# First layer of a two-layer network with a PEER expert layer: all 128 expert columns multiplied ahead of the value pass, sums of the value pass in eight PSUM banks

## The chip, the cores and the metric

The kernel runs on one core of a Trainium2 chip. The metric is the time of one execution on the device in microseconds (us), as the median over runs; a profile of one execution shows what each engine did. The engines are TensorE (PE, with its weight loads as PEld), VectorE (DVE), ScalarE (ACT), GpSimd (POOL) and SyncE (SP), which only issues transfers (DMA).

## The reference, cut to what matters

Each of two layers has a mixer part and then an expert part (PEER). The change lies in the expert part:

```python
q = (t @ wq).reshape(TOKEN_BLOCK, PEER_HEADS, 2, PEER_DK // 2)
s = jnp.einsum("thpd,hpnd->thpn", q, sub_keys)
st, it = lax.top_k(s, PEER_TOPK)
...
best, pos = lax.top_k(cand, PEER_TOPK)
e = jnp.take_along_axis(cidx, pos, axis=-1)
g = jax.nn.softmax(best, axis=-1)
u = jnp.take(eu, e, axis=0)
act = jax.nn.gelu(jnp.einsum("thkd,td->thk", u, t), approximate=False)
return jnp.einsum("thk,thkd->td", g * act, jnp.take(ev, e, axis=0))
```

There are 128 x 128 experts of width 1024. The first layer handles 512 tokens (256 context, 256 latent), the second only the 256 latent ones. Each layer's modulation vectors are silu(c) @ ada_w + ada_b.

## The kernel before, in words

Nothing is gathered. The experts are taken as 128 columns of 128 experts, and every column is computed for every token; a dense matrix G of gate weights, zero where an expert was not chosen, picks what counts. Three steps follow one another in a layer:

- **Routing** (`route`): the top-16 searches on DVE (phase 0), then the spread (phase 1), which makes G out of one-hot products: 128 steps in the first layer, each with one-hots from ACT, DVE and POOL, four short matmuls (L836) and two reductions on DVE (L838) into `rt_stg`, which goes to DRAM as G.
- **Inner products** (`inner`): for an expert column j the weights `u` are loaded, split into a high and a low part (`uh` on ACT, `ul` on POOL, L869 and L870) and multiplied with the split activations in three passes: 24 matmuls of 128x512 per column in the first layer (L887 to L889) into the PSUM tile `h`, then a gelu into a `ga` tile (L893). Columns below `NPRE` are woven into the routing: one each `EVERY` steps; their results go to DRAM (`act`).
- **Value pass** (`outer`): 64 steps of two columns. `weights` loads the gelu results back (`ga<-act`, tiles with three buffers), multiplies them with G (L965, DVE), and splits the product into `wh` (L968, ACT) and `wl` (L969, DVE). `values` loads the value rows `v` (two buffers) and splits them into `vh` (ACT) and `vl` (POOL for columns below `NPRE` in the first layer, else DVE). `second` multiplies: 512 tokens are four blocks `tt`, 1024 features two halves `k`, three passes, so 24 matmuls per column. Sums of blocks 0 and 1 stay in four PSUM banks (`acc`); those of blocks 2 and 3 go through two PSUM buffers (`f`) and are added on DVE to `accS` in SBUF (L1007). In the first layer columns 104 to 127 have their inner products here. `finish` turns each sum over, adds it to `x` and takes sums of squares.

While the first layer's value pass runs, `side` computes seven modulation vectors: 56 loads `wa`, each read by two DVE instructions `wtr` (L196), 112 in all. Each engine works its instructions off in a fixed order, and SP issues all these transfers in a fixed order too; a scheduler makes these orders from the program.

In the second layer 256 tokens make two blocks; all sums are in four banks already, and POOL has no part in the value pass.

Of the kernel before, what the change touches and what calls it, by code (L numbers as in the profile page):

```python
# [7 lines left out]
F32 = mybir.dt.float32  # L8
# [8 lines left out]
D = 1024  # L17
# [6 lines left out]
SPLIT = 3072.0  # L24
TG = 32
TT = 512
NPRE = (104, 96)
EVERY = ((3, 2), (2, 1))
UB = (5, 8)
UR = (2, 4)  # L30
VB = (5, 6)
# [18 lines left out]
class Net:  # L50
# [137 lines left out]
    def ada(self, l, P, w, cb, src):  # L188

        red = self.red()  # L190
        for b in range(NB):
            wt = self.wts.tile([128, D], F32, name="wa", tag="wt", bufs=2)
            self.nc.sync.dma_start(wt, src[b])
            for s in range(2):
                trash = self.wts.tile([128, D], BF, name="wtr", tag="whi", bufs=WB)
                self.nc.vector.scalar_tensor_tensor(trash, wt, 1.0, cb[:, s], op0=OP.mult, op1=OP.mult,  # L196
                                                    accum_out=red[:, b, s:s + 1])
            yield
        self.ada_out(l, P, w, red)

    def ada_half(self, l, P, w, acc, tags, banks, ctag):
# [694 lines left out]
    def peer(self, l, P, h, c0, npre, side):  # L896
        nc, I, tc = self.nc, self.I, self.tc
        n = TT - c0
        per = 512 // n
        NG = n // TG  # L900
        Gd = self.dram.tile([128, NG, 128, TG], F32, name=f"G{l}")
        Ad = self.dram.tile([npre // per, 128, 512], F32, name=f"act{l}")
        S = {}
        ups = ExitStack()
        pool = ups.enter_context(tc.tile_pool(name=f"expu{l}", bufs=2))
        with ExitStack() as rs:
            self.psum = rs.enter_context(tc.tile_pool(name=f"psr{l}", bufs=5, space=bass.MemoryType.PSUM))
            self.pbufs = {"f": 5}
            self.iotap = self.psum.tile([128, 128], F32, name="iotap", bufs=1)
            nc.vector.tensor_copy(self.iotap, self.iota)  # L910
            self.routep = rs.enter_context(tc.tile_pool(name=f"route{l}", bufs=1))
            def early():
                for j in range(npre):
                    a = self.inner(l, h, c0, j, per, pool, S, nc.gpsimd if LO[l][j % len(LO[l])] == "p" else nc.vector)
                    if a is not None:
                        nc.sync.dma_start(Ad[j // per], a)
                    yield
            pre = early()
            k = 0
            for phase in self.route(l, h, c0, Gd):  # L920
                if phase is None:
                    for _ in range(MORE[l]):
                        next(pre, None)
                    continue
                k += 1
                if k % EVERY[l][phase] == 0:
                    next(pre, None)
            for _ in pre:
                pass
        with ExitStack() as vs:  # L930
            self.psum = vs.enter_context(tc.tile_pool(name=f"psv{l}", bufs=2, space=bass.MemoryType.PSUM))
            self.pbufs = {"f": 2}
            X = vs.enter_context(tc.tile_pool(name=f"expv{l}", bufs=2))
            if l == 0:
                self.adap = vs.enter_context(tc.tile_pool(name="adap", bufs=1))
            self.outer(l, P, h, c0, npre, Gd, Ad, pool, X, S, side)
        ups.close()

    def outer(self, l, P, h, c0, npre, Gd, Ad, pool, X, S, side):
# [2 lines left out]
        per = 512 // n  # L942
        nt = n // 128
        V = I["peer_v"][l].rearrange("(i j) d -> i j d", j=128)
        acc = [self.psum.tile([128, 512], F32, name=f"acc{k}", tag=f"acc{k}", bufs=1) for k in range(4)]
        accS = X.tile([128, 4, 512], F32, name="accS", bufs=1) if nt > 2 else None
        st = {}

        def weights(n2):
# [21 lines left out]
                    r.append((wh[:, k * n:(k + 1) * n], wl[:, k * n:(k + 1) * n]))  # L971
            st["w", n2] = r

        def values(n2):
            r = []
            for j in (2 * n2, 2 * n2 + 1):
                v = X.tile([128, D], F32, name="v", tag="v", bufs=VR[l])
                nc.sync.dma_start(v, V[:, j, :])
                r.append(self.usplit(v, "v", X, VB[l], nc.gpsimd if j < npre and nt > 2 else nc.vector))
            return r  # L980

        def second(n2):
            vs = values(n2)
            ws = st.pop(("w", n2))
            order = [(tt, k) for tt in range(nt) for k in range(2)]
            if nt > 2:
                order = [(tt + d, k) for tt in (0, 1) for k in range(2) for d in (2, 0)]
            if n2 == last:
                order = [(tt, k) for tt in ((2, 0, 3, 1) if nt > 2 else (0, 1)) for k in range(2)]
            for tt, k in order:  # L990
                t = slice(tt * 128, tt * 128 + 128)
                if tt < 2:
                    A, s0, s1 = acc[2 * tt + k], n2 == first, n2 == last
                else:
                    A, s0, s1 = self.ps(), True, True
                for jj in range(2):
                    vh, vl = vs[jj][k]
                    wh, wl = ws[jj]
                    nc.tensor.matmul(A, wh[:, t], vh, start=s0 and jj == 0, stop=False)  # L999
                    nc.tensor.matmul(A, wh[:, t], vl, start=False, stop=False)  # L1000
                    nc.tensor.matmul(A, wl[:, t], vh, start=False, stop=s1 and jj == 1)  # L1001
                if tt >= 2:
                    o = accS[:, 2 * (tt - 2) + k]
                    if n2 == first:
                        nc.vector.tensor_copy(o, A)
                    else:
                        nc.vector.tensor_add(o, o, A)  # L1007
                if n2 == last:
                    finish(tt, k)

        def finish(tt, k):

            s = 0 if c0 + tt * 128 >= T else 1
            t = slice(c0 + tt * 128, c0 + tt * 128 + 128)
            sq = self.wts.tile([128, 512], F32, name="sq", tag="wlo", bufs=WB)
            if k == 0:
                st["ss", tt] = self.psum.tile([128, 128], F32, name="ss", tag="h", bufs=2)
            ss = st["ss", tt]
            if tt < 2:
                o = pool.tile([128, 512], F32, name="ga", tag="ga", bufs=3)  # L1020
                nc.scalar.activation(o, acc[2 * tt + k], AF.Copy)
            else:
                o = accS[:, 2 * (tt - 2) + k]
            pt = self.ps()
            for c in range(4):
                nc.tensor.transpose(pt[:, c * 128:(c + 1) * 128], o[:, c * 128:(c + 1) * 128], self.ident)
            for c in range(4):
                xs = self.x[:, 4 * k + c, t]
                nc.vector.scalar_tensor_tensor(xs, pt[:, c * 128:(c + 1) * 128],
                                               P["mod"][:, 5 * NB + 4 * k + c, s:s + 1], xs, op0=OP.mult, op1=OP.add)  # L1030
            nc.scalar.activation(sq.rearrange("p (c t) -> p c t", c=4), self.x[:, 4 * k:4 * k + 4, t], AF.Square)
            for c in range(4):
                nc.tensor.matmul(ss, self.ones, sq[:, c * 128:(c + 1) * 128], start=k + c == 0, stop=k + c == 4)
            eng = nc.vector if tt else nc.gpsimd
            if l == DEPTH - 1:
                if k == 0:
                    st["ys", tt] = self.wts.tile([128, NB, 128], F32, name="ys", tag="wt", bufs=2)
                ys = st["ys", tt]
                b = slice(4 * k, 4 * k + 4)
                eng.tensor_mul(ys[:, b], self.x[:, b, t], self.fg[:, b, None].to_broadcast([128, 4, 128]))  # L1040
            if k == 0:
                return
            self.rsqrt(ss, 1.0 / D, self.rsx[:, t], sq[:, :128])
            if l == DEPTH - 1:
                for b in (slice(0, 4), slice(4, 8)):
                    eng.tensor_mul(ys[:, b], ys[:, b], self.rsx[:, None, t].to_broadcast([128, 4, 128]))
                    nc.sync.dma_start(self.out[:, b, tt * 128:tt * 128 + 128], ys[:, b])
# [6 lines left out]
        for k in range(65):  # L1054
# [4 lines left out]
            if k < 64:  # L1059
                n2 = seq[k]  # L1060
                for j in (2 * n2, 2 * n2 + 1):
                    if j >= npre:
                        a = self.inner(l, h, c0, j, per, pool, S, nc.gpsimd if nt > 2 else nc.vector)
                        if a is not None:
                            st["a", j // per] = a
                weights(n2)
            if k:
                second(seq[k - 1])
            next(side, None)
            if k % 4 == 0:  # L1070
                next(side, None)


    def run(self):
# [111 lines left out]
```

## Time and profile before

| | us |
|---|---|
| median of 3 runs (lowest, highest) | 3119.13 (3117.34, 3130.06) |
| the profiled execution, own time | 3119.87 |
| its span in the trace | 3118.2 |
| PE busy in the span | 2933.3 (94%) |
| DVE, ACT, POOL busy | 2233.9, 1440.0, 1378.2 |

The span runs from the first to the last recorded instruction; 1.7 us of the execution lie around it. Busy shares are means over stages that differ; the rows below are read stage by stage. The first layer's routing takes some 430 to 1112 us of the span, its value pass 1127 to 2022, the second layer's value pass 2660 to 3110.

### The profile page before, as it was taken

The page shows a single profiled execution, that of the slowest core. Times are in us where ns is not written, and L with a number is a line of the kernel's source. Part 1 is how long each engine was busy: PE and PEld are TensorE (multiplying, and loading weights), DVE is VectorE, ACT ScalarE, POOL GpSimd, SP SyncE. Part 2 cuts the span into 40 slices and gives each one's busy share as a digit, 9 for nine tenths or more (in the row PEclk, how much of TensorE's full clock was granted, in tenths as well). Part 3 has the DMA queues.
Part 4 walks back from the last instruction along what each step waited for, and adds up shares of the span by engine and source line. Part 5 has one row for each costly group of instructions (what it writes and reads, how often), then busy time and mean ns, then how long its engine had stood idle before and what let it go on. Part 6 is the DMA issues. An engine that isn't in the chain of part 4 may idle for free.

```text
span 3118.2 us, 43562 instructions
## 1 busy us (share of the span) xinstructions
PE 2933.3 (94%) x14930; PEld 2424.5 (78%) x14930; DVE 2233.9 (72%) x4604; ACT 1440.0 (46%) x2861; POOL 1378.2 (44%) x1079
## 2 busy tenths in 40 slices
PE   7899989999999978989999999978989998999998
PEld 4476578888888856767888888867689998788887
DVE  7987637867777769998555545486759789666665
ACT  4345443346666632223333333345455765555554
POOL 4434245656666645343434334163478875000000
PEclk9999999999999989999999999989999999999999
DMA  6511124345655577776555555121255876987874
GB/s 225 176 48 55 39 82 137 123 146 182 209 207 208 208 237 254 239 239 213 174 174 169 179 154 180 41 87 51 67 172 170 274 257 234 314 267 256 260 229 136
DMA packets 249806, 550.95 MB, mean 177 GB/s; under 512 B 17440, under 2 KB 118304, under 8 KB 246384
## 3 DMA queue, kind: packets, MB, share of 16 engines
q1 hardware_dynamic: 248864, 545.74, 53.3%
q8 instruction: 118, 1.93, 0.3%
q0 software_dynamic: 720, 2.43, 0.2%
q14 instruction: 104, 0.85, 0.1%
HBM read 456.87 MB, written 91.23 MB: 176 GB/s over the span
## 4 chain that ended last, share of the span: by engine, by line
PE 64%; DVE 13%; DMA 5%; issue 2%; ACT 1%; POOL 1%; SPq 0%; DVEq 0%; ACTq 0%; POOLq 0%
PE h L887 9%; PE h L888 9%; PE h L889 9%; PE acc L1000 6%; PE acc L999 5%; PE acc L1001 5%; PE f L836 3%; DVE wtr L196 3%; PE f L999 3%; PE f L1000 3%; PE f L1001 3%; DMA ga<-act 1%; DMA v<-in_peer_v 1%; DVE cy L491 1%; DMA u<-in_peer_u 1%
## 5 line engine op out<-in xcount | busy, mean ns | idle before, releaser
L870 POOL TENSOR_TENSOR ul<-u,uh 128x512 fp32r<-128x512 f32 x448 | 594.8, 1339 | 382.9 <-ACT uh L869 370.5
L887 PE MATMUL h<-hh,uh 128*128 128x512 f32 (+1 forms) x2048 | 694.4, 339 | 3.2 <-DVE rt_stg L838 2.1
L889 PE MATMUL h<-hh,ul 128*128 128x512 f32 (+1 forms) x2048 | 691.2, 338 | 5.1 <-POOL ul L870 5.1
L888 PE MATMUL h<-hl,uh 128*128 128x512 f32 (+1 forms) x2048 | 691.5, 338 | 0.0
L869 ACT ACTIVATE vh<-v 128x512 fp32r<-128x512 f32 x512 | 319.5, 628 | 590.1 <-PE acc L1001 368.3
L869 ACT ACTIVATE uh<-u 128x512 fp32r<-128x512 f32 x512 | 318.4, 628 | 468.2 <-PE h L888 320.8
L870 POOL TENSOR_TENSOR vl<-v,vh 128x512 fp32r<-128x512 f32 x208 | 303.3, 1470 | 366.5 <-ACT vh L869 357.3
L889 PEld LDWEIGHTS h<-hh,ul 128*128 128x128 f32 x2048 | 391.0, 191 | 46.7 <-POOL ul L870 5.8
L887 PEld LDWEIGHTS h<-hh,uh 128*128 128x128 f32 x2048 | 391.3, 191 | 45.4 <-DVE rt_stg L838 2.7
L888 PEld LDWEIGHTS h<-hl,uh 128*128 128x128 f32 x2048 | 391.4, 191 | 38.0
L1000 PE MATMUL acc<-vl,wh 128*128 128x512 f32 x1024 | 402.5, 393 | 4.3 <-DVE vl L870 4.1
L999 PE MATMUL acc<-vh,wh 128*128 128x512 f32 x1024 | 401.6, 392 | 1.5 <-ACT vh L869 1.5
L1001 PE MATMUL acc<-vh,wl 128*128 128x512 f32 x1024 | 400.6, 391 | 0.0
L241 POOL TENSOR_TENSOR wlo<-wt,whi 128x512 fp32r<-128x512 f32 x164 | 248.1, 1524 | 246.4 <-ACT whi L240 224.5
L838 DVE TENSOR_REDUCE rt_stg<-f 128x256 f32<-128x512 f32 x384 | 243.6, 687 | 137.4 <-PE f L836 136.6
L965 DVE TENSOR_TENSOR ga<-ga,g 128x512 f32<-128x512 f32 x192 | 163.2, 856 | 177.4 <-DMA ga<-act 99.6
L870 DVE TENSOR_TENSOR vl<-v,vh 128x512 fp32r<-128x512 f32 x304 | 205.6, 693 | 107.4 <-ACT vh L869 107.1
L999 PE MATMUL f<-vh,wh 128*128 128x512 f32 x512 | 205.1, 401 | 44.8 <-DVE accS L1007 34.3
L1000 PEld LDWEIGHTS acc<-vl,wh 128*128 128x128 f32 x1024 | 193.7, 189 | 49.2 <-DVE vl L870 9.2
L1007 DVE TENSOR_TENSOR accS<-accS,f 128x512 f32<-128x512 f32 x252 | 171.3, 680 | 83.0 <-PE f L1001 82.9
L999 PEld LDWEIGHTS acc<-vh,wh 128*128 128x128 f32 x1024 | 193.9, 189 | 42.5 <-ACT vh L869 2.2
L1001 PEld LDWEIGHTS acc<-vh,wl 128*128 128x128 f32 x1024 | 193.6, 189 | 40.2
(320 smaller groups left out, 5372.1 us busy)
## 6 DMA issues: line engine op xcount, KB each, us to landing
u<-in_peer_u SPq DMA_DIRECT2D x256, 512.0 KB, 4.1
v<-in_peer_v SPq DMA_DIRECT2D x256, 512.0 KB, 4.4
G<-rt_stg SPq DMA_DIRECT2D x24, 2048.0 KB, 7.0
act<-ga SPq DMA_DIRECT2D x152, 256.0 KB, 3.4
ga<-act SPq DMA_DIRECT2D x152, 256.0 KB, 4.2
g<-G SPq DMA_DIRECT2D x32, 1024.0 KB, 6.2
wa<-in_ada_t SPq DMA_DIRECT2D x56, 512.0 KB, 4.2
w<-in_ada_w SPq DMA_DIRECT2D x20, 1024.0 KB, 6.4
```

Source lines behind the costliest of these rows:

```text
L241: nc.gpsimd.tensor_sub(lo, raw, hi)
L838: nc.vector.tensor_reduce(stg[:, :, t4 + k2:t4 + k2 + 2].rearrange("p j t -> p t j"), pg.rearrange("p (t x j) -> p t j x", t=2, x=2), axis ...
L869: nc.scalar.activation(hi, raw[:, k * 512:(k + 1) * 512], AF.Copy)
L870: lo_eng.tensor_sub(lo, raw[:, k * 512:(k + 1) * 512], hi)
L887: nc.tensor.matmul(o, uh, hh[:, c, c0:], start=c == 0, stop=False)
L888: nc.tensor.matmul(o, uh, hl[:, c, c0:], start=False, stop=False)
L889: nc.tensor.matmul(o, ul, hh[:, c, c0:], start=False, stop=c == NB - 1)
L965: nc.vector.tensor_mul(av, av, g)
L999: nc.tensor.matmul(A, wh[:, t], vh, start=s0 and jj == 0, stop=False)
L1000: nc.tensor.matmul(A, wh[:, t], vl, start=False, stop=False)
L1001: nc.tensor.matmul(A, wl[:, t], vh, start=False, stop=s1 and jj == 1)
L1007: nc.vector.tensor_add(o, o, A)
```

## The change

All 128 columns of the first layer are multiplied ahead of the value pass (`NPRE` 128); in the spread they come at 5 of 8 steps in place of 4 of 8 (`RATE`), and what is left over follows the spread. The value pass of the first layer has no inner products, and its sums take eight PSUM banks, two per block, for the whole pass; `accS` and its additions are gone. The low parts `vl` are all made on DVE. `second` goes column by column. In `finish` all sums leave through ACT, and the banks just emptied take the transposes and the sums of squares. `side` stops after each of the two `wtr` instructions of a load, is called twice a step, and its instructions are held at their place in the program.

```diff
-NPRE = (104, 96)
-EVERY = ((3, 2), (2, 1))
+NPRE = (128, 96)
+RATE = (((1, 3), (5, 8)), ((1, 2), (1, 1)))
...
-                self.nc.vector.scalar_tensor_tensor(trash, wt, 1.0, cb[:, s], op0=OP.mult, op1=OP.mult,
-                                                    accum_out=red[:, b, s:s + 1])
-            yield
+                self.tc.keep_in_program_order(self.nc.vector.scalar_tensor_tensor(
+                    trash, wt, 1.0, cb[:, s], op0=OP.mult, op1=OP.mult, accum_out=red[:, b, s:s + 1]))
+                yield
...
-                if k % EVERY[l][phase] == 0:
+                a, b = RATE[l][phase]
+                if k * a // b > (k - 1) * a // b:
                     next(pre, None)
...
-        acc = [self.psum.tile([128, 512], F32, name=f"acc{k}", tag=f"acc{k}", bufs=1) for k in range(4)]
-        accS = X.tile([128, 4, 512], F32, name="accS", bufs=1) if nt > 2 else None
+        bank = lambda k: self.psum.tile([128, 512], F32, name=f"acc{k}", tag=f"acc{k}", bufs=1)
+        acc = [bank(k) for k in range(2 * nt)]
...
+            for jj in range(2):
+                vs = values(2 * n2 + jj)
+                wh, wl = ws[jj]
+                s0, s1 = n2 == first and jj == 0, n2 == last and jj == 1
+                order = (2, 0, 3, 1) if s1 and nt > 2 else range(nt)
+                for tt in order:
+                    t = slice(tt * 128, tt * 128 + 128)
+                    for k in range(2):
+                        A = acc[2 * tt + k]
+                        vh, vl = vs[k]
+                        nc.tensor.matmul(A, wh[:, t], vh, start=s0, stop=False)
+                        nc.tensor.matmul(A, wh[:, t], vl, start=False, stop=False)
+                        nc.tensor.matmul(A, wl[:, t], vh, start=False, stop=s1)
+                        if s1:
+                            finish(tt, k)
...
-            if tt < 2:
-                o = pool.tile([128, 512], F32, name="ga", tag="ga", bufs=3)
-                nc.scalar.activation(o, acc[2 * tt + k], AF.Copy)
+            o = pool.tile([128, 512], F32, name="ga", tag="ga", bufs=3)
+            nc.scalar.activation(o, acc[2 * tt + k], AF.Copy)
+            if nt > 2:
+                pt = bank(2 * tt + k)
+                if k == 1:
+                    st["ss", tt] = bank(2 * tt)[:, :128]
...
                 weights(n2)
+                next(side, None)
             if k:
                 second(seq[k - 1])
             next(side, None)
-            if k % 4 == 0:
-                next(side, None)
```

Where the change moves instructions, the order of the built programs shows it. Numbers behind a name tell one tile from the next. First VectorE, early in the first layer's value pass, before: `ga` is the product with G, `wl` a low part of it, `accS` an addition into SBUF, `wtr` a modulation instruction.

```order
L965 TENSOR_TENSOR ga_10964<-ga_10964,g_10962 128x512
L969 TENSOR_TENSOR wl_10870<-ga_10866,wh_10869 128x512
L196 SCALAR_TENSOR_TENSOR wtr_11056,red_10665<-wa_11054,cb_10657 128x1024
L969 TENSOR_TENSOR wl_10877<-ga_10873,wh_10876 128x512
L1007 TENSOR_TENSOR accS_10640<-accS_10640,f_10900 128x512
L196 SCALAR_TENSOR_TENSOR wtr_11058,red_10665<-wa_11054,cb_10657 128x1024
L196 SCALAR_TENSOR_TENSOR wtr_11062,red_10665<-wa_11060,cb_10657 128x1024
L1007 TENSOR_TENSOR accS_10640<-accS_10640,f_10914 128x512
L965 TENSOR_TENSOR ga_10971<-ga_10971,g_10962 128x512
L196 SCALAR_TENSOR_TENSOR wtr_11064,red_10665<-wa_11060,cb_10657 128x1024
L1007 TENSOR_TENSOR accS_10640<-accS_10640,f_10928 128x512
```

The same engine in the changed program, a pair of columns from the steady part of the pass (`vl` is a low part of the values; a `ga` tile takes the buffer of the third `ga` before it, so ga_12119 that of ga_11948, ga_12126 that of ga_12031):

```order
L970 TENSOR_TENSOR wl_11952<-ga_11948,wh_11951 128x512
L196 SCALAR_TENSOR_TENSOR wtr_11955,red_11580<-wa_11937,cb_11572 128x1024
L196 SCALAR_TENSOR_TENSOR wtr_12027,red_11580<-wa_12025,cb_11572 128x1024
L870 TENSOR_TENSOR vl_12050<-v_12047,vh_12049 128x512
L966 TENSOR_TENSOR ga_12119<-ga_12119,g_12029 128x512
L870 TENSOR_TENSOR vl_12054<-v_12047,vh_12053 128x512
L970 TENSOR_TENSOR wl_12035<-ga_12031,wh_12034 128x512
L870 TENSOR_TENSOR vl_12084<-v_12081,vh_12083 128x512
L966 TENSOR_TENSOR ga_12126<-ga_12126,g_12029 128x512
L870 TENSOR_TENSOR vl_12088<-v_12081,vh_12087 128x512
L970 TENSOR_TENSOR wl_12042<-ga_12038,wh_12041 128x512
```

And the pair behind it (ga_12209 takes the buffer of ga_12038, ga_12216 that of ga_12119):

```order
L196 SCALAR_TENSOR_TENSOR wtr_12045,red_11580<-wa_12025,cb_11572 128x1024
L196 SCALAR_TENSOR_TENSOR wtr_12117,red_11580<-wa_12115,cb_11572 128x1024
L870 TENSOR_TENSOR vl_12138<-v_12135,vh_12137 128x512
L870 TENSOR_TENSOR vl_12142<-v_12135,vh_12141 128x512
L970 TENSOR_TENSOR wl_12123<-ga_12119,wh_12122 128x512
L870 TENSOR_TENSOR vl_12172<-v_12169,vh_12171 128x512
L966 TENSOR_TENSOR ga_12209<-ga_12209,g_12207 128x512
L966 TENSOR_TENSOR ga_12216<-ga_12216,g_12207 128x512
L870 TENSOR_TENSOR vl_12176<-v_12169,vh_12175 128x512
L970 TENSOR_TENSOR wl_12130<-ga_12126,wh_12129 128x512
```

The additions are gone, four `vl` have come, and of the `wtr` there are two per pair of columns, where before four stood in eleven rows. Second, the queue of SP in the changed program, over the same two pairs:

```order
L977 DMA v_12081<-in_peer_v 128x1024
L960 DMA ga_12119<-act0_3118 128x512
L193 DMA wa_12115<-in_ada_t 128x1024
L977 DMA v_12135<-in_peer_v 128x1024
L960 DMA ga_12126<-act0_3118 128x512
L954 DMA g_12387<-G0_3117 128x16x128
L977 DMA v_12169<-in_peer_v 128x1024
L193 DMA wa_12203<-in_ada_t 128x1024
L960 DMA ga_12209<-act0_3118 128x512
L960 DMA ga_12216<-act0_3118 128x512
L977 DMA v_12225<-in_peer_v 128x1024
```

Two of the four `ga` loads stand directly behind a `v` load. Third, ScalarE where the spread has ended, in the changed program (L893 is a gelu, here those of the last four columns; `sg` belongs to `side`):

```order
L893 ACTIVATE ga_11420<-h_11387 128x512
L184 ACT_TABLE_LOAD
L184 ACTIVATE sg_11574<-cb_11572 128x1024
L869 ACTIVATE uh_11506<-u_11499 128x512
L184 ACTIVATE sg_11577<-cb_11572 128x1024
L893 ACT_TABLE_LOAD
L893 ACTIVATE ga_11458<-h_11425 128x512
L869 ACTIVATE vh_11603<-v_11601 128x512
L893 ACTIVATE ga_11496<-h_11463 128x512
L869 ACTIVATE vh_11693<-v_11691 128x512
L893 ACTIVATE ga_11534<-h_11501 128x512
L969 ACTIVATE wh_11561<-ga_11558 128x512
```

Before, two inner columns stood on TensorE between the last short matmul of the spread and the first of the value pass; now seven do, and the first weights of the value pass (wh_11561) follow the last gelus, whose tiles hold the three `ga` buffers.

## Rows read from the trace of the kernel before

**Rows 1.** Busy time by stretch: us, busy (instructions) per engine, clock, DMA share, GB/s
```profile
690.00:1103.40 413.40, 412.69 (x2051) 350.48 (x2050) 310.75 (x596) 276.62 (x673) 285.29 (x194) 1.00 0.58 201
1103.40:1127.00 23.60, 16.83 (x65) 13.25 (x63) 7.23 (x13) 4.87 (x11) 7.42 (x6) 0.78 0.65 223
1127.00:1460.00 333.00, 283.40 (x1154) 222.05 (x1154) 310.99 (x427) 97.16 (x162) 150.23 (x85) 0.94 0.74 242
1460.00:2004.00 544.00, 543.86 (x2399) 449.82 (x2398) 284.16 (x366) 176.22 (x295) 210.65 (x163) 1.00 0.52 161
2660.00:3100.00 440.00, 434.16 (x2232) 369.47 (x2231) 283.21 (x438) 233.01 (x392) 0.00 (x0) 1.00 0.76 248
```

**Rows 2.** Groups by line, 1127 to 1460 us: busy, mean ns, idle before
```profile
L196 DVE SCALAR_TENSOR_TENSOR wtr<-wa,cb 128x1024 bf16<-128x1024 f32 x112 | 174.2, 1574 | 3.8 <-DMA wa<-in_ada_t 3.8
L870 POOL TENSOR_TENSOR vl<-v,vh 128x512 fp32r<-128x512 f32 x72 | 127.6, 1789 | 130.3 <-ACT vh L869 121.6 <-DMA v<-in_peer_v 8.7
L999 PE MATMUL f<-vh,wh 128*128 128x512 f32 x169 | 71.4, 422 | 44.8 <-DVE accS L1007 34.3 <-ACT vh L869 10.5
...
L1007 DVE TENSOR_TENSOR accS<-accS,f 128x512 f32<-128x512 f32 x80 | 54.1, 677 | 0.0
L965 DVE TENSOR_TENSOR ga<-ga,g 128x512 f32<-128x512 f32 x47 | 42.0, 908 | 24.4 <-DMA cb<-in_cond 17.1 <-DMA ga<-act 6.2 <-issue 1.1
L969 DVE TENSOR_TENSOR wl<-ga,wh 128x512 fp32r<-128x512 f32 x44 | 37.2, 869 | 1.0 <-ACT wh L968 0.5 <-PE acc L1000 0.3
```

**Rows 3.** TensorE in order of time, 1111 to 1146 us: start, us
```profile
1111.05 1.19 PE L836 MATMUL f<-rt_oh_g,rt_oh_i 128*128 128x256 f32 x4 [3.01 <-DVE rt_oh_i L832]
...
1137.54 0.80 PE L999 MATMUL f<-vh,wh 128*128 128x512 f32 x1 [10.46 <-ACT vh L869]
...
1145.39 0.63 PE L1000 MATMUL acc<-vl,wh 128*128 128x512 f32 x1
1145.82 0.63 PE L1001 MATMUL acc<-vh,wl 128*128 128x512 f32 x1
```

**Rows 4.** Groups by line, 2660 to 3100 us, second layer, POOL idle
```profile
L870 DVE TENSOR_TENSOR vl<-v,vh 128x512 fp32r<-128x512 f32 x256 | 172.0, 689 | 78.2 <-ACT vh L869 77.9
L969 DVE TENSOR_TENSOR wl<-ga,wh 128x512 fp32r<-128x512 f32 x64 | 43.9, 687 | 10.9 <-ACT wh L968 10.8
L965 DVE TENSOR_TENSOR ga<-ga,g 128x512 f32<-128x512 f32 x64 | 43.6, 689 | 31.8 <-DMA ga<-act 19.9 <-ACT ga L893 10.1 <-DMA g<-G 1.7
```

**Rows 5.** VectorE in order of time, 1300 to 1311 us
```profile
1299.99 0.69 DVE L870 TENSOR_TENSOR vl<-v,vh 128x512 fp32r<-128x512 f32 x1 [0.35 <-ACT vh L869]
1300.60 0.69 DVE L965 TENSOR_TENSOR ga<-ga,g 128x512 f32<-128x512 f32 x1
...
1309.79 1.21 DVE L196 SCALAR_TENSOR_TENSOR wtr<-wa,cb 128x1024 bf16<-128x1024 f32 x1
1310.94 0.08 DVE L196 DVE_READ_ACCUMULATOR wtr<-wa,cb 128x1 f32 x1
```

**Rows 6.** SP's issues in order of time, 1612 to 1615 us
```profile
1612.90 0.32 SPq L959 DMA_DIRECT2D ga<-act  x1
1614.05 0.33 SPq L978 DMA_DIRECT2D v<-in_peer_v  x1
1614.61 0.32 SPq L959 DMA_DIRECT2D ga<-act  x1
```

**Rows 7.** VectorE in order of time, 1616 to 1620 us
```profile
1616.15 1.08 DVE L965 TENSOR_TENSOR ga<-ga,g 128x512 f32<-128x512 f32 x1 [0.97 <-DMA ga<-act]
...
1619.40 0.69 DVE L965 TENSOR_TENSOR ga<-ga,g 128x512 f32<-128x512 f32 x1 [1.57 <-DMA ga<-act]
```

**Rows 8.** Transfers, 2700 to 3050 us, second layer: count, KB each, median us to landing
```profile
ga<-act SPq DMA_DIRECT2D x40, 256.0 KB, 5.4
```

**Rows 9.** VectorE in order of time, end of the first layer's value pass
```profile
2007.56 1.12 DVE L1029 SCALAR_TENSOR_TENSOR x<-f,mod,x 128x128 f32<-128x128 f32 x4 [0.75 <-PE f L1026]
...
2031.67 0.29 DVE L263 SCALAR_TENSOR_TENSOR rsx<-sq,rsx 128x128 f32<-128x128 f32 x1
```

More of the change, by code (lines that the diff above doesn't have):

```diff
@@ L972, in weights, with values @@
             st["w", n2] = r
[L974 to L980, printed above, removed]
+        def values(j):
+            v = X.tile([128, D], F32, name="v", tag="v", bufs=VR[l])
+            nc.sync.dma_start(v, V[:, j, :])
+            return self.usplit(v, "v", X, VB[l], nc.vector)
@@ L982, in second @@
         def second(n2):
-            vs = values(n2)
             ws = st.pop(("w", n2))
[L985 to L991, printed above, removed]
-                if tt < 2:
[L993 to L1009, printed above, removed]
@@ L1015, in finish @@
             sq = self.wts.tile([128, 512], F32, name="sq", tag="wlo", bufs=WB)
[L1016 to L1019, printed above, removed]
-                o = pool.tile([128, 512], F32, name="ga", tag="ga", bufs=3)
-                nc.scalar.activation(o, acc[2 * tt + k], AF.Copy)
-            else:
-                o = accS[:, 2 * (tt - 2) + k]
-            pt = self.ps()
+            o = pool.tile([128, 512], F32, name="ga", tag="ga", bufs=3)
[4 more added lines that the diff above has]
+                    st["ss", tt] = bank(2 * tt)[:, :128]
+            else:
+                pt = self.ps()
+                if k == 0:
+                    st["ss", tt] = self.psum.tile([128, 128], F32, name="ss", tag="h", bufs=2)
             for c in range(4):
@@ L1031, in finish @@
             nc.scalar.activation(sq.rearrange("p (c t) -> p c t", c=4), self.x[:, 4 * k:4 * k + 4, t], AF.Square)
-            for c in range(4):
-                nc.tensor.matmul(ss, self.ones, sq[:, c * 128:(c + 1) * 128], start=k + c == 0, stop=k + c == 4)
+            st["sq", tt, k] = sq
+            if nt == 2 or k == 1:
+                ss = st["ss", tt]
+                for b in (range(2) if nt > 2 else (k,)):
+                    for c in range(4):
+                        nc.tensor.matmul(ss, self.ones, st["sq", tt, b][:, c * 128:(c + 1) * 128],
+                                         start=b + c == 0, stop=b + c == 4)
             eng = nc.vector if tt else nc.gpsimd
@@ L1062, in outer @@
                     if j >= npre:
-                        a = self.inner(l, h, c0, j, per, pool, S, nc.gpsimd if nt > 2 else nc.vector)
+                        a = self.inner(l, h, c0, j, per, pool, S, nc.vector)
                         if a is not None:
```

## The prediction

> **What bounds the kernel now.** I read the stretches first, then the groups by line inside the one that loses time, then single waits. Between 1460 and 2004 us TensorE is busy 543.86 of 544 us and does 2399 matmuls, so one costs 0.2268 us [rows 1]; that is its pace whenever operands are there, and nothing in the change takes a matmul away. The spread up to 1103 us is as full (412.69 of 413.4), and so is the second layer's value pass (434 of 440) [rows 1]: there is little to win in either. The loss lies between. From 1127 to 1460 us only 1154 matmuls are done, which at 0.2268 us are 261.7 us; 71.3 of the 333 us are lost. From 1103.4 to 1127 us, the border of spread and value pass, 65 matmuls are at most 14.7 us of 23.6, another 8.9 lost, at a granted clock of 0.78 [rows 1]. Together **80 us**, the most that a change of the first layer's value pass can give.
>
> The 71 us have two causes. At the border TensorE waits 10.46 us for the first `vh`, and 8 us later its matmuls are still 0.43 us apart, the spacing of the lower clock level, 1.2 GHz, against 0.227 at 2.4 GHz [rows 3]. After that it waits for DVE: 34.3 us for `accS`, which empties the two buffers `f` [rows 2]. DVE is busy 311 of 333 us there, because all 112 `wtr` have been drawn into these 333 us (174 us of work), and because it works beside POOL: `wtr` takes 1574 ns where the undisturbed ones take about 1210 [rows 2, 5], `ga` 908 and `wl` 869 where they take 689 and 687 in the second layer, with POOL idle [rows 2, 4].
>
> **The change part by part.**
>
> *Inner columns.* 24 columns of 24 matmuls, 576 x 0.2268 = 131 us of TensorE, go ahead of the value pass. TensorE is the bound at either place, so this moves time and saves none. In the spread DVE and POOL are busy 311 and 285 of 413 us [rows 1], and with the added matmuls the stage gets longer than their added work (two `ul` per column on POOL, about the size of its `vl`, 1.79 us [rows 2], beside 24 x 0.2268 = 5.4 us of TensorE): taken at 0. If that cover were gone, POOL's 24 x 3.6 = 86 us would show. The 48 added transfers of gelu results lie in the same shade.
>
> *No additions in SBUF.* 256 instructions of 677 ns [rows 2], 173 us of DVE, go, and with them the wait for `f`. In exchange 208 `vl` come from POOL, 208 x 0.69 = 143 us [rows 4]. POOL then rests in the whole pass, so the slow `ga`, `wl` and `wtr` become those of rows 4 and 5.
>
> *`wtr` held in place.* Two per pair of columns, over 56 of 64 pairs, in place of four in a pair's time: the 34.3 us of waiting for DVE have no cause of this kind left.
>
> *The new wait.* What DVE does per pair is now fixed by the order: eight instructions of 128x512, which follow each other by 0.61 us, and two `wtr`, 1.15 us apart [rows 5]: 8 x 0.61 + 2 x 1.15 = 7.2 us. TensorE needs 48 x 0.2268 = 10.9 us. DVE has 3.7 us to spare, and spends them on `ga` loads. A `ga` buffer comes free with a `wl`, SP then issues the next load into it, and the product waits for the landing. In the order shown the work between the freeing `wl` and the product that waits is: for ga_12119 two `wtr` and a `vl`, 2.9 us; for ga_12126 one `vl`, 0.6; for ga_12209 two `wtr` and four others, 4.7; for ga_12216 a `vl` and a `ga`, 1.2. Everything behind a product on DVE waits too, the `vl` that TensorE needs next among it, and behind a late `vl` the next `v` load. How long a load takes until the product starts, two pairs of rows say. Issued at 1612.90 with the queue clear, the product starts at 1616.15: 3.25 us. Issued at 1614.61, 0.56 us behind a `v` load of twice the size, it starts at 1619.40: 4.79 us [rows 6, 7].
>
> Per two pairs DVE thus needs 2 x 7.2 = 14.4 us and its waits; TensorE 21.8.
> - All loads clear (3.25): waits 0.35 + 2.65 + 0 + 2.05 = 5.0, sum 19.4. TensorE stays the bound, cost 0.
> - All behind a transfer (4.79): 1.9 + 4.2 + 0.1 + 3.6 = 9.8, sum 24.2, 2.4 over; times 28 (56 pairs) 67 us.
> - What I take: ga_12119 and ga_12126 directly behind a `v` load, as SP's order has them (4.79); ga_12216 in the middle, 4.0, since G, `v` and `wa` loads stand shortly ahead. Waits 1.9 + 4.2 + 2.8 = 8.9, sum 23.3, 1.5 over, 42 us; with ga_12216 clear (2.05) 22.5, 0.7 over, 21 us. I take the mean, **32 us**.
>
> *The border.* Before, 25 us lay between the spread's last matmul and the first value matmul, two columns in them [rows 3]; now seven columns, 7 x 24 x 0.2268 = 38 us, hide G, `v` and the first splits, so the 10.46 us go. New is that the last three gelus hold the `ga` buffers: the first weight can be loaded only when the gelu of the third to last column has been written out, and by then SP stands behind the store of the next. Its landing, the product and `wh` come about when TensorE runs out, the load being 3.25 us [rows 6, 7], the store an estimated as much, and a column 5.4. I take **8 us**: 4 idle and 4 at the lower clock. Bounds 0 and the 19 of before (10.46, and 8 us at half pace with two short waits).
>
> *The end.* `finish` runs inside the last column, not the last pair: 32 updates of `x` at 0.28 us and 16 root instructions at 0.29 [rows 9] are 13.6 us of DVE behind 5.4 us of matmuls in place of 10.9. Before, this took from 2007.56 to 2031.67 us with idle times of DVE in it [rows 9]. **4 us** more, bounds 0 and 5.5.
>
> *Second layer.* Order by column in place of by pair; TensorE is full there, so 0 (bounds -3 and +3).
>
> *Sum.* -80 + 32 + 8 + 4 = -36 us. The profiled execution took 3119.87 us, 0.7 above the median: 3119.9 - 36 = **3084 us**.
>
> **The rivals.**
>
> *TensorE bound throughout.* If the loads land clear, the 32 us fall away: 3119.9 - 80 + 12 = 3052 us, 3044 without border cost. For it: SP issues ga_12126 when `wl` has waited for TensorE, and the `v` load ahead may be through by then; and DVE had 98% of its time filled in the bad stretch yet waited only 6.2 us for `ga` [rows 2]. Against: the load in rows 6 that stood in this same place took 4.79. The Trainium skill, page "DMA: Bandwidth & Descriptors", section "Anatomy of one DMA", gives a transfer about 2.0 us fixed and its bytes at 436 GB/s (fitted on GpSimd's path); an estimate from that page for 256 KB is 2.6 us, and by it this rival would be the case. The trace does not agree where a load follows another: 4.79 us.
>
> *The waits take it all back.* With all loads at 4.79 the gain is 80 - 67 - 12 = 1 us: 3119 us. The added `wa` load per pair, now through the whole pass, speaks for it: the share of the transfer engines was 0.52 after 1460 us and 0.74 with `wa` [rows 1].
>
> *Slower: a crowded queue.* In the second layer, at a share of 0.76, the median `ga` load took 5.4 us [rows 1, 8]. With 5.4 throughout: waits 2.5 + 4.8 + 0.7 + 4.2 = 12.2, sum 26.6, 4.8 over, times 28 134 us, and the kernel takes 3119.9 - 80 + 134 + 12 = 3186 us. It decides from about 4.8 us per load on. Against it: the second layer moved the same bytes in less time (248 GB/s), while a DVE that is late also asks for less.
>
> **How the numbers follow.** The likeliest case, 3060 to 3104 us around 3084, gets 0.45; TensorE bound (3044 to 3060) 0.22; gain taken back (3104 to 3135) 0.20; slower (above 3135) 0.13. A measurement of this kernel can tell about 0.5%, 16 us, from no change: faster 0.67, same 0.20, slower 0.13. The range 3046 to 3140 leaves out about 2 in 10.
>
> **What would show it.** In the profile after: no wait of TensorE for `accS`; `wtr` near 1.21 us and spread over the pass; POOL empty in it; `ga` products as DVE's largest wait, with `DMA ga<-act` as releaser, and TensorE's small waits ended by `vl`. A value pass of 697 us (3072 x 0.2268) would show the first rival, over 765 us the second. The prediction would be wrong if DVE's order let TensorE run dry in another way, by `v` loads with their two buffers above all, or if the longer spread waited for POOL.

## The result, and the profile after

The changed kernel takes 3081.89 us (median of 4 runs, 3078.09 to 3089.23) where the kernel before takes 3118.24: a ratio of 0.988, 95% interval 0.9848 to 0.9913, 36 us less. The profiled execution has a span of 3076.4 us, 41.8 less than before's.

The stretches of the changed kernel first, as in [rows 1]: busy time and instructions per engine, the granted clock, the transfer share, GB/s.

```profile
300.00:340.00 40.00, 37.77 (x147) 21.88 (x146) 33.08 (x73) 21.30 (x57) 7.61 (x9) 1.00 0.04 14
690.00:1141.00 451.00, 451.00 (x2199) 381.44 (x2198) 281.22 (x535) 275.40 (x648) 295.82 (x204) 1.00 0.54 193
1141.00:1165.00 24.00, 24.00 (x120) 20.36 (x120) 18.44 (x36) 15.46 (x37) 15.03 (x11) 1.00 0.44 154
1300.00:1600.00 300.00, 291.82 (x1245) 230.54 (x1244) 189.12 (x314) 87.58 (x156) 0.00 (x0) 1.00 0.68 226
2725.00:3045.00 320.00, 320.00 (x1663) 275.79 (x1662) 208.29 (x324) 168.84 (x288) 0.00 (x0) 1.00 0.75 247
```

The spread keeps TensorE full with the added columns in it. In the value pass POOL is empty, and TensorE is not full: from 1300 to 1600 us it does 1245 matmuls, at 0.2268 us 282.4 of 300 us. What it waits for is in the waits of the middle of the pass, 1260 to 1890 us (engine and line, what it waits for, us in total, times, longest):

```profile
ACT vh L869 <- DMA v<-in_peer_v: 415.8, 101, 8.5
DVE ga L966 <- DMA ga<-act: 145.5, 82, 5.2
DVE vl L870 <- ACT vh L869: 92.3, 27, 4.3
PEld acc L993 <- DVE vl L870: 45.7, 71, 1.6
PE acc L993 <- DVE vl L870: 15.9, 34, 1.2
```

This is the picture that the prediction drew: no `accS`, VectorE waiting longest for `ga` loads, TensorE for the `vl` that stands behind. VectorE's groups in the same stretch show that POOL no longer slows it: `wtr` 1218 ns for 1574 in [rows 2], the product 692 for 908, `wl` 683 for 869.

```profile
L870 DVE TENSOR_TENSOR vl<-v,vh 128x512 fp32r<-128x512 f32 x216 | 146.4, 685 | 92.3 <-ACT vh L869 92.3
L196 DVE SCALAR_TENSOR_TENSOR wtr<-wa,cb 128x1024 bf16<-128x1024 f32 x107 | 126.8, 1218 | 0.0
L966 DVE TENSOR_TENSOR ga<-ga,g 128x512 f32<-128x512 f32 x109 | 74.8, 692 | 145.8 <-DMA ga<-act 145.5
L970 DVE TENSOR_TENSOR wl<-ga,wh 128x512 fp32r<-128x512 f32 x108 | 73.8, 683 | 0.0
```

Where the 41.8 us of span come from, taken from the first and last matmul of each stage in the two traces:

| stage | before | after | difference | forecast |
|---|---|---|---|---|
| spread and columns behind it, less 119.8 for the 528 matmuls moved there | 422.1 | 411.6 | -10.4 | -8.9 |
| TensorE idle at the border | 10.5 | 4.5 | -5.9 | -6.5 |
| lost in the value pass (its length less 0.2268 us per matmul) | 67.7 | 53.9 | -13.8 | -20.8 |
| everything else | | | -11.6 | 0 |

(The forecast of the third row is -71.3 + 10.5 for what was lost, +32 for the new wait, +4 for the clock at the border and +4 for the end.)

### The profile page after: what moved, and what is told of

It is laid out like the page before. It is cut to its first block, busy times and chain, and to the rows that moved or that the text cites. A ratio compares the mean times of both kernels' runs of the same rounds, so it can differ in the third digit from the quotient of the medians.

```text
span 3076.4 us, 43429 instructions
## 1 busy us (share of the span) xinstructions
PE 2923.6 (95%) x14930; PEld 2407.8 (78%) x14930; DVE 2088.7 (68%) x4556; ACT 1428.0 (46%) x2865; POOL 1064.0 (35%) x871
## 4 chain that ended last, share of the span: by engine, by line
PE 57%; DMA 14%; DVE 12%; issue 2%; ACT 2%; POOL 1%; SPq 0%; DVEq 0%; ACTq 0%; POOLq 0%
DMA ga<-act 11%; PE h L887 10%; PE h L888 10%; PE h L889 10%; PE acc L993 6%; PE acc L994 5%; PE acc L992 5%; PE f L836 3%; DVE vl L870 2%; DVE wl L970 1%; DVE cy L491 1%; PE f L333 1%; DMA u<-in_peer_u 1%; PE f L334 1%; PE f L335 1%
## 5 line engine op out<-in xcount | busy, mean ns | idle before, releaser
L993 PE MATMUL acc<-vl,wh 128*128 128x512 f32 x1536 | 609.4, 397 | 21.2 <-DVE vl L870 19.1
L992 PE MATMUL acc<-vh,wh 128*128 128x512 f32 x1536 | 599.6, 390 | 6.5 <-ACT wh L969 4.5
L994 PE MATMUL acc<-vh,wl 128*128 128x512 f32 x1536 | 599.9, 391 | 0.2
L870 DVE TENSOR_TENSOR vl<-v,vh 128x512 fp32r<-128x512 f32 x512 | 343.9, 686 | 179.5 <-ACT vh L869 178.7
L993 PEld LDWEIGHTS acc<-vl,wh 128*128 128x128 f32 x1536 | 288.5, 188 | 113.0 <-DVE vl L870 55.5
L992 PEld LDWEIGHTS acc<-vh,wh 128*128 128x128 f32 x1536 | 288.8, 188 | 68.4 <-ACT wh L969 4.9
L994 PEld LDWEIGHTS acc<-vh,wl 128*128 128x128 f32 x1536 | 288.9, 188 | 58.9 <-DVE wl L970 1.6
L966 DVE TENSOR_TENSOR ga<-ga,g 128x512 f32<-128x512 f32 x192 | 131.8, 691 | 217.7 <-DMA ga<-act 201.3
L824 DVE SCALAR_TENSOR_TENSOR rt_oh_g<-iotap,rt_sT,rt_sg 128x256 fp32r<-128x256 f32 x512 | 213.2, 474 | 0.1
L240 ACT ACTIVATE whi<-wt 128x512 fp32r<-128x512 f32 x164 | 100.5, 627 | 162.4 <-PE f L320 71.2
```

The lines of the kernel that those rows point to most:

```text
L824: nc.vector.scalar_tensor_tensor(og[:, k], self.iotap[:, None, :].to_broadcast([128, 2, 128]), sT[:, 1, c:c + 1], sg[:, c, :, None].bitcas ...
L870: lo_eng.tensor_sub(lo, raw[:, k * 512:(k + 1) * 512], hi)
L966: nc.vector.tensor_mul(av, av, g)
L992: nc.tensor.matmul(A, wh[:, t], vh, start=s0, stop=False)
L994: nc.tensor.matmul(A, wl[:, t], vh, start=False, stop=s1)
```

## Experiments

Twelve kernels ran, each beside the kernel before on the same chip; ratios to it are compared. "Lost" is the length of the value pass in the profile of a run less 3072 x 0.2268 = 696.7 us (3600 matmuls where inner products lie in it).

**Is it the number of buffers, or the queue?** Four kernels, all edits of the changed one.

```
# own3, own6: loads of gelu results in a pool of their own, 3 or 6 buffers (first layer)
-    a = pool.tile([128, 512], F32, name="ga", tag="ga", bufs=3)
+    a = X.tile([128, 512], F32, name="ga", tag="gw", bufs=6)
# v3
-VR = (2, 3)
+VR = (3, 3)
# nowa: one wa tile, loaded once, read by all wtr
```

> The changed kernel with six buffers of their own for the gelu results that the first layer's value pass loads back, in place of three shared with the inner products; nothing else differs. Theory (the `ga` loads pace VectorE: three buffers let a load start only when the low part two columns earlier is done): the value pass falls from 750.6 us to some 705 (floor 3072 x 0.2268 = 697), the border from 4.5 us to under 2, the time from 3082 to about 3035. Rival V (the `v` loads with two buffers are what is late; `vh` waited 416 us for them on ScalarE): the pass stays at 735 or above, the time at 3065 or above. Rival Q (the queue is too crowded for any number of buffers): the pass stays near 750, `ga` loads take longer than their 4.7 us.

> The changed kernel with the loads of gelu results in three buffers of their own, apart from those of the inner products: the number that the value pass has is the same, only the border is freed. Theory: the border falls from 4.5 us to under 2, the value pass stays within 5 us of 750.6; the time is about 3078. Whoever puts the loss of the pass down to the border expects it to fall with it, by 20 us or more.

> The changed kernel with three buffers for `v` in place of two, the `ga` buffers as they are. Theory (the `ga` loads pace VectorE): the pass stays at 740 us or above, since a `vl` that stands behind a waiting product gains nothing from an early `vh`; time 3072 or more. Rival V (the two buffers of `v` are the cause): the pass falls to some 705 us, the time to about 3036. Rival Q (the queue): the pass near 750.

> The changed kernel with one `wa` load in place of 56; the 112 `wtr` all read that one tile, so the modulation is not the reference's. VectorE's work and order stay, the queue carries 512 of 2560 KB per pair less. Theory: `ga` loads come down from 4.7 us towards 3.25, the waits per two pairs from 8.9 to about 5 us, and the pass to 700 to 715 us; the time to 3035 to 3047. Rival V says the same if `v` loads get shorter. Whoever holds the fixed order of VectorE and the three buffers alone responsible, whatever a load takes, expects 740 or more.

Measured: ratios 0.9901 (0.9884 to 0.9917), 0.9902 (0.9882 to 0.9922), 0.9898 (0.9882 to 0.9915) and 0.9904 (0.9886 to 0.9921). None is faster than the changed kernel (0.988), and none lost less than its 53.9 us: lost 68.1, 65.8, 57.1 and 60.7 us. My theory of three buffers fell with own6: VectorE still waited 154.9 us for `ga` loads. Rival Q's sign came there too (the median `ga` load took 5.8 us, after 4.7); what speaks against a queue too crowded is nowa, and pinmul below, which moves more bytes per us without the loss. v3 turned the wait round (ScalarE waits 347.2 us for TensorE and 87.1 for `v`, which was 415.8) and left the loss: VectorE then waited 238.2 us for `ga`, and none for `vh`. nowa took away a fifth of the bytes, and the median `ga` load stayed at 4.73 us, after 4.67, where the expectation had it near 3.25: the bytes of `wa` do not set the load's time. Half of own3's expectation held: with buffers of its own (own3, own6) the border falls from 4.5 to 0.74 us, and the first pair takes 11.03 us in place of 12.70. Its pass was to stay within 5 us of 750.6 and took 762.5 us; the loss of the pass is not the border's.

**Both at once, and another queue.**

```
# own6v3: own6 and v3 together
# own6pool: own6, the load issued by POOL in the first layer
-    nc.sync.dma_start(a, Ad[bank])
+    nc.gpsimd.dma_start(a, Ad[bank])
```

> The changed kernel with both at once: six buffers for the loaded gelu results and three for `v`. Either alone left the pass at 754 to 765 us, with VectorE still 155 to 238 us on `ga` loads. Theory 2 (two loops close through VectorE's order: a `v` or a `ga` load, some 3.9 us until it has landed, the product, `vl`, `wl`, 0.6 each, and then the issue that this frees; together some 5.9 us per column where TensorE needs 5.44; SP issues `v` and `ga` in one line, so each of the two shortages holds the other's load up too): only with both freed does the pass fall, to 712 us or less, the time to about 3040 beside the 3091 of the single edits. Rival S (the loads themselves, 6 to 8 us whenever the 1 MB of G is ahead of them): pass 730 to 750. Rival D (VectorE's order as such): no change.

> The changed kernel with six buffers for the loaded gelu results, whose loads POOL issues instead of SP, so that they no longer stand behind `v` loads that wait for one of two buffers; `v` keeps its two. Theory 2 (a `ga` load is late because it stands behind a `v` issue in SP's line): the pass falls to 720 us or less, the time to some 3045. Whoever sees the cause in the two `v` buffers themselves expects 750 us; whoever sees it in the transfers (6 to 8 us behind G) expects 735 or more.

Measured: own6v3 0.9921 (0.9902 to 0.9941), lost 64.9 us; own6pool 1.0374 (1.0355 to 1.0392), lost 216 us, a clear miss. Theory 2 fell too. The waits of own6v3, 1260 to 1890 us:

```profile
ACT vh L869 <- PE acc L995: 395.0, 107, 7.2
DVE ga L967 <- DMA ga<-act: 244.6, 106, 5.2
PEld acc L994 <- DVE vl L870: 58.4, 73, 2.7
```

With buffers to spare, 106 products waited 106 times. own6pool shows why, in POOL's only group of that stretch (busy, mean ns, idle before):

```profile
L961 POOL DMA_DIRECT2D ga<-act x87 | 47.5, 546 | 584.7 <-DVE wl L971 584.7
```

Six buffers, and still every load stands waiting for a `wl` to free one: the scheduler had used the added buffers to put loads *and their products* further ahead. The distance between a load and its product, which is what VectorE waits for, hardly grew. From the issue of a load to the start of its product it took 4.8 us in the changed kernel (median, 1260 to 1890 us), 6.0 in own6 and 5.8 in own6v3, and landing took 4.7, 5.8 and 5.7 us of that. Why issuing from POOL costs 216 us and not some 65 was not followed. The built orders say the same of own6: in the changed kernel 92 of the 128 products stand ahead of the `wl` of two columns that come before their own, in own6 89 stand ahead of five.

**The place of the product.** The loop can be read in the changed kernel. VectorE, 1520 to 1528 us:

```profile
1520.58 0.69 DVE L966 TENSOR_TENSOR ga<-ga,g 128x512 f32<-128x512 f32 x1 [1.17 <-DMA ga<-act]
1521.19 0.68 DVE L870 TENSOR_TENSOR vl<-v,vh 128x512 fp32r<-128x512 f32 x1
1521.79 0.68 DVE L970 TENSOR_TENSOR wl<-ga,wh 128x512 fp32r<-128x512 f32 x1
1522.39 0.68 DVE L870 TENSOR_TENSOR vl<-v,vh 128x512 fp32r<-128x512 f32 x1
1526.46 0.70 DVE L966 TENSOR_TENSOR ga<-ga,g 128x512 f32<-128x512 f32 x1 [3.38 <-DMA ga<-act]
```

And SP's issues there:

```profile
1521.90 0.33 SPq L977 DMA_DIRECT2D v<-in_peer_v  x1
1522.50 0.33 SPq L960 DMA_DIRECT2D ga<-act  x1
```

`vl` ends at 1521.87 and SP issues the next `v`; `wl` ends at 1522.47 and SP issues the next `ga` load; that load is what the next product in VectorE's order needs, 3.9 us later. From product to product it takes 5.88 us, without a `wtr` between them, and TensorE needs 5.44 us per column. The test holds the product back instead of giving it more room:

```
# late6: six buffers, loads (G's too) written a pair of columns ahead, and
+    mul = nc.vector.tensor_mul(av, av, g)
+    if l == 0:
+        tc.keep_in_program_order(mul)
# shortwtr: wtr over wt[:, :64]
```

> The changed kernel with six buffers for the loaded gelu results, each load written a pair of columns ahead of its product, and the product held at its place in the order of the program. In all kernels so far the product stands on VectorE right behind the place where its load was reckoned to land, and more buffers only moved load and product forward together: the last `v` issue ahead of the load, the load, the product. Theory 3 (it is this order that makes VectorE wait, and behind it `vl` and TensorE): the waits for `ga` loads fall from 150 to 245 us to under 40, the pass from 754 to 765 us to 715 or less, the time from some 3091 to about 3045. Rival V (two `v` buffers then hold up `vh` and `vl` as much): the pass stays at 730 or above.

> The changed kernel with `wtr` over 64 of 1024 elements, so that the modulation is not the reference's; loads, order and waits stay. VectorE has some 2 us less to do per pair of columns. Theory 3 (the loss is the time from a load's issue to its landing, in a loop through VectorE's order, 5.9 us per column without any `wtr` in it): the pass loses some 0.9 us per pair still, 735 us or more. Rival W (VectorE's work is what is too long in a pair): the pass falls to 710 us or less, the time to some 3045.

late6: 3033.57 us, ratio 0.9722 (0.9705 to 0.9739). Every pair of columns but the first and last takes 10.88 us, 48 x 0.2268; lost 8.1 us. Its waits, 1260 to 1890 us, and VectorE in order of time:

```profile
ACT vh L869 <- PE acc L1003: 430.1, 116, 4.0
DVE vl L870 <- ACT vh L869: 214.7, 115, 3.2
ACT vh L869 <- DMA v<-in_peer_v: 2.1, 7, 0.5
```

```profile
1502.11 0.69 DVE L973 TENSOR_TENSOR ga<-ga,g 128x512 f32<-128x512 f32 x1
1502.72 0.68 DVE L870 TENSOR_TENSOR vl<-v,vh 128x512 fp32r<-128x512 f32 x1
1504.05 0.69 DVE L870 TENSOR_TENSOR vl<-v,vh 128x512 fp32r<-128x512 f32 x1 [0.65 <-ACT vh L869]
1504.66 0.68 DVE L979 TENSOR_TENSOR wl<-ga,wh 128x512 fp32r<-128x512 f32 x1
1505.26 0.68 DVE L973 TENSOR_TENSOR ga<-ga,g 128x512 f32<-128x512 f32 x1
```

No product waits any more. VectorE now waits for `vh`, which waits for TensorE to free its buffers: the waits follow TensorE and no longer hold it up. The loads did not get faster (median 4.6 us), but a product starts 27.1 us (median) after its load was issued.

shortwtr: 0.9777 (0.976 to 0.9795), lost 14.5 us: rival W's numbers, not theory 3's. But it doesn't settle for W, because the scheduler made another order of it: in the changed kernel the two products of a pair stand directly behind each other in 29 of 64 pairs, here in 56, which makes one loop per pair out of two. Its last pairs, behind the modulation, have the two places again. The stretches of shortwtr:

```profile
1528.00:1850.00 322.00, 322.00 (x1422) 266.62 (x1421) 160.37 (x360) 103.92 (x179) 0.00 (x0) 1.00 0.72 240
1850.00:1908.00 58.00, 56.70 (x242) 44.56 (x241) 23.86 (x38) 18.26 (x33) 0.00 (x0) 1.00 0.53 171
```

1422 matmuls in 322 us are the full pace; 242 in 58 us are 3.1 us short in some five pairs, though VectorE has no `wtr` there and the transfers are fewest. The order makes loss without `wtr`; what a long `wtr` adds in the same order, this run can't say.

**Is the product's place enough, and what was it in the kernel before?**

```
# pinmul: the changed kernel, the product held in place (the + lines above), nothing else
# pin: the kernel before with the change's part on the modulation alone
# pinpinmul: pin, and the product held in place
# nopin: the changed kernel without the change's part on the modulation
```

> The changed kernel with one edit: in the first layer the product of the loaded gelu results with G is held at its place in the order of the program; the three shared `ga` buffers, the loads and the two `v` buffers stay. If the order on VectorE alone made the loss (theory 3, as the run with the load a pair ahead has it), this is enough: a buffer is freed by `wl` three columns, 16 us, ahead of the product that needs it again; the pass falls to 710 us or less, the border stays at 4.5, the time is 3034 to 3042. If buffers and the earlier load were needed too, the waits for `ga` stay above 60 us and the pass at 725 or above.

> The kernel before with orders alone: `wtr` held in place, two per pair, and the product with G held in place; four banks, additions into SBUF, 104 columns ahead and POOL's `vl` stay. With `wtr` alone held the pass lost 72 us. Theory E (the loss of the kernel before is VectorE's order too): the loss falls below 45 us, the time to 3095 or less. Rival F (the additions through two `f` buffers are too tight beside `wtr` and a busy POOL, whatever the order): the time stays within 10 us of before, 3112 or more, and TensorE still waits 40 us or more for the additions.

> The kernel before with the change's part on the modulation alone: `wtr` held in place, two per pair of columns; four banks, additions into SBUF, 104 columns ahead and `vl` on POOL as before. If the crowding of VectorE at the start of the pass was the loss (the prediction's second cause), VectorE has 7.2 to 9.5 us of work per pair beside 10.9, the wait for the additions goes, and the loss falls from 78 us with the border to about 35: some 40 us less than before the change, as much as the whole change brought. If the additions and two `f` buffers were the loss, it stays within 10 us of before.

> The changed kernel without its part on the modulation: the `wtr` are free to move and a step asks for as many as before the change. In this program's order they stand 4.5 to a pair over the first 25 pairs, in place of 2 over 56. Theory A (VectorE's loops with the loads carry each `wtr` that stands in them): about 3 us over per pair, 80 us in the first 25 pairs and 10 behind, some 35 us more than the changed kernel, as slow as before the change. Theory B (the `wtr` fill time in which VectorE waits for loads anyway): the time stays within 10 us of the changed kernel's.

pinmul: 3037.51 us, ratio 0.9731 (0.9717 to 0.9744), lost 9.9 us, border 4.25 us, as expected: three buffers, the same loads, one instruction of each column held in place. All 128 products now stand behind the `wl` of every earlier column (5 of them did in the changed kernel), and a product starts 10.8 us (median) after its load was issued, where landing takes 4.2. SP's issues stand in another order too, so it is this distance, and not the edit alone, that shows the cause. pinmul is the version to keep; it and late6 beat both kernels, and late6's further 4 us are about the border's. Its stretch, and its VectorE group from 1260 to 1890 us:

```profile
1300.00:1600.00 300.00, 300.00 (x1325) 248.51 (x1324) 203.08 (x340) 92.81 (x165) 0.00 (x0) 1.00 0.77 243
...
L966 DVE TENSOR_TENSOR ga<-ga,g 128x512 f32<-128x512 f32 x116 | 79.4, 684 | 0.0
```

In the kernel before the same orders do little. pin: 1.001 (0.9996 to 1.0023), lost 71.7 us. The crowd of `wtr` is gone, and up to 1460 us 31.8 us are lost where it was 61.0 (border not counted), but behind it 39.9 are lost where it was 6.7. pinpinmul: 0.9972 (0.9954 to 0.9989), lost 53.5 us. Rival F holds in its main point, that it stays close to before, though its 40 us were too many: TensorE's first wait in pinpinmul, over the whole pass, is

```profile
PE f L1001 <- DVE accS L1009: 27.8, 21, 4.2
```

So something else of the change had to go with it before the order could pay: the additions with their two `f` buffers, by TensorE's longest wait, though POOL's `vl` went at the same time and no kernel parts the two. And the order has to be mended before the change pays in full: 1.2% for the change, 2.7% with the product in place.

nopin: 0.995 (0.9932 to 0.9968), lost 70.8 us, 17 more than the changed kernel: between the two theories. Its stretches with 4.5 `wtr` to a pair, and behind them:

```profile
1300.00:1540.00 240.00, 223.48 (x952) 177.71 (x951) 197.02 (x338) 69.69 (x124) 0.00 (x0) 0.99 0.84 267
1550.00:1905.00 355.00, 338.87 (x1436) 265.73 (x1436) 149.93 (x240) 100.44 (x180) 0.00 (x0) 1.00 0.56 177
```

952 matmuls (19.8 pairs) are 215.9 of 240 us, 1.2 us short per pair where theory A said 3: most of a `wtr` does fall into time in which VectorE waits. And 1436 (29.9 pairs) are 325.7 of 355 us, 0.98 us short per pair or 29.3 us in all, without any `wtr` and with `wa` gone from the queue. This is about the 0.9 us per pair of theory 3, without the `wtr` that rival W blames.

## Why the prediction was right, and where only its sum was

*Where the loss was and what the change removes.* Right. The border and the tail of the spread gave 10.4 + 5.9 us, forecast 8.9 + 6.5. With POOL out of the pass VectorE's instructions took the times of [rows 4, 5].

*The cover of the inner columns.* Right: TensorE is busy 475 of 475 us from 690 to 1165 us.

*`wtr` held in place.* The step said that no cause of the 34.3 us would be left. pin shows that holding them does nothing by itself, and nopin that it is worth some 17 us of the pass once the additions are gone.

*The new wait.* Its place was right, its size in part by luck. VectorE was to wait 8.9 us per two pairs for `ga`; from 1260 to 1890 us, some 54 pairs, it waited 145.5 + 92.3 = 237.8 us, 8.8 per two pairs, but only 5.4 of them for `ga`: the waits for `vh` had not been forecast. TensorE lost 43.7 us by it (pairs 2 to 63) where 32 was taken: the 42 us that the working had first given, before it was averaged with a kinder case, was the better figure. The 3.25 us of a clear load did not hold: there a load took 3.5 us at least, and 6.2 in the median when G was under way with it. The loop described is in the trace (SP waited for a `wl` before 79 of its 108 `ga` issues there). But the three buffers were not what kept it closed, since six of them changed nothing; it was the place of the product in VectorE's order.

*The border and the end.* Of the 8 us, 4.5 idle and 1.8 in the first pair; own3 shows that these are the price of the three shared `ga` buffers, as said. The end cost nothing, where 4 was taken: the last pair lies 8.4 us over its matmuls, after 6.9 lost behind 1460 us before, but from the last value matmul to the second layer's first inner product it takes 290.4 us, after 292.6.

*What lay outside.* 11.6 us were not in the sum at all. From the stages alone the time would have come to 3119.9 - 30.2 = 3089.7, 6 us above the forecast, since the pass gave 7 us less than was taken. 5.75 us lie ahead of the routing, in instructions that are the same and stand in the same order in both programs: the kernel before did 130 matmuls from 300 to 340 us at a granted clock of 0.87, the changed one 147 at 1.00. That is chance: in ten traces with the same instructions in the same order up to there, the first inner product starts between 454.4 and 465.6 us. About 7.7 us lie in the second layer's value pass, forecast at 0 with bounds of 3: 433.5 us, after 441.2. That is no chance: the eleven kernels with the second layer in columns took 432.8 to 434.9, the three in pairs 440.9 to 441.6. Some 3.3 us of it are given back at its two ends, and 2.2 us are the shorter way behind the first layer's pass. The stretches of the kernel before that answer to the first and last rows above:

```profile
300.00:340.00 40.00, 37.77 (x130) 21.12 (x129) 30.01 (x65) 18.79 (x51) 7.59 (x9) 0.87 0.04 14
2760.00:3080.00 320.00, 317.79 (x1640) 271.79 (x1639) 208.12 (x321) 170.10 (x285) 0.00 (x0) 1.00 0.77 250
```

Why the order by columns fills those 2.2 us of 320 was not tried.

*The rivals.* The first, 3052 us with loads that land clear, was nearer to what can be had than to what happened: late6 and pinmul reach 3034 and 3038 us, with loads that take 4.6 and 4.2 us (median) to land. One of its arguments was misread: VectorE's time in the bad stretch was filled to 93%, 311 of 333 us [rows 1], not 98%. The estimate beside it, 2.6 us by the Trainium skill, page "DMA: Bandwidth & Descriptors", section "Anatomy of one DMA", is about what the fastest `ga` loads of the kernel before took (2.53 us at least in its value pass); from 1260 to 1890 us of the changed kernel none landed in under 3.5 us.

## What to carry to other kernels

When an engine waits for loads in a fixed order, ask first where the waiting instruction stands, and only then how many buffers there are: here the scheduler spent each added buffer on moving load and user forward together, and the wait stayed. Holding the one instruction that needs the load at its place in the program was worth 1.5%, while the edits of buffers and queues gained nothing. And check a forecast's sum against its stages: here the stages gave 6 us less than forecast and 11.6 us came from outside them, so that the total came out close is luck.

## What the runs showed of the hardware

- A `ga` load issued 0.6 us behind a `v` load of twice its size lands 0.7 us behind it: `v` issued at 1521.90 took 3.80 us, `ga` issued at 1522.50 took 3.87. Of the 108 `ga` loads from 1260 to 1890 us in the changed kernel, the 53 issued while a 1 MB load of G was under way took 6.2 us in the median (4.4 to 7.8), the other 55 took 3.8 (3.5 to 5.0). Taking the 512 KB `wa` loads out of the queue did not shorten the median (4.73 us, after 4.67).
- What POOL beside it costs VectorE can be read inside one kernel, the one before, in its first value pass. The 45 `wtr` with no POOL instruction beside them took 1215 ns in the mean, the 67 with one 1816; products 689 and 1199, `wl` 685 and 1026. The additions `accS`, which read PSUM, took 679 and 682.
- The first inner product starts between 454.4 and 465.6 us in the ten traces in which every engine has the same instructions ahead of it: 11 us, 0.4 per cent of the time, which a single profiled span can't tell from an edit.
